# A hybrid trunk of two layers: bias sums and products with ones moved five matmuls up, and one matmul behind each widened to 258 columns

## The chip, the cores and the metric

The kernel runs on one core of a Trainium2 chip. The metric is the device time of one execution in microseconds (us). Three runs of the kernel before took 574.57, 574.65 and 574.93 us; the median is 574.65 us.

## The reference

Two layers work on 256 tokens of width 1024. Each layer is a token mixer with a residual, then an MLP with a residual, and each begins with an RMS norm. Layer 0 mixes by latent attention (MLA, 8 heads, rotary key), layer 1 by block-sparse attention (MoBA, here one block of 256 keys) with a relative bias from a table of 32 buckets. The MLP is `relu(h @ w_in)` squared, times `w_out`, with 4096 hidden columns.

```python
def sq_relu_mlp(h, w_in, w_out):
    a = jax.nn.relu(h @ w_in)
    return (a * a) @ w_out

for i in range(DEPTH):
    h = rms_norm(x, attn_norm[i])
    x = x + (mla_mixer(h, ...) if i % 2 == 0 else moba_mixer(h, ..., positions, rel_bias_table))
    h = rms_norm(x, mlp_norm[i])
    x = x + sq_relu_mlp(h, mlp_w_in[i], mlp_w_out[i])
```

The relative bias depends on positions and the table alone, so it can be computed at any time ahead of layer 1's attention.

## The kernel before, in words

**Arithmetic.** Weights and activations are float32. TensorE multiplies them as fp32r, in one pass, which keeps fewer bits; so each operand is split into a high part and the rest (`wh`, `wl` for weights, `hTh`, `hTl`, `a0`, `a1`, `aT0`, `aT1` for activations), and each product is three matmuls: high by high, rest by high, high by rest. This is `mm3` (lines 87 to 91), which calls `mm` (line 85, where the profile puts nearly all matmuls). ScalarE makes the high part (line 149), VectorE the rest (line 158), for units of 128x1024 of the weights that the DMA queue of SyncE brings in the order of use (line 138). `fill` asks for the next units, `done` gives one free.

**Layout.** Activations are kept transposed, 128 features by 256 tokens. In the MLPs and in the output projections of the attention the weight part (128x128) is the stationary operand, and the 256 tokens are the moving one, so each matmul has 256 columns and sums into a PSUM bank. In the projections ahead of the attention it is the other way: the tokens are stationary, and 512 columns of the weights (384 or 320 in the first) move.

**The attention's end.** `run_heads` computes eight heads and their output projection. The last three of its columns, `col(5)` to `col(7)`, run behind everything else: 3 x 8 heads x 3 = 72 matmuls of 256 columns each, one group of 24 after the other.

**The MLP.** `mlp` (line 870) runs twice over half of the hidden columns (`r`), and in each: eight times `first` (`j` from 0 to 7), which makes two blocks of 128 hidden columns with 2 x 8 `mm3` = 48 matmuls, then eight times an output block (`d`), 16 `mm3` = 48 matmuls into one bank. That makes 32 groups of 48 per MLP. Behind a group come `fill`, then what the list `fillers` has for that place (lines 890 and 931), then the reading of the bank: ScalarE and VectorE square it (lines 896 to 904), or VectorE scales it (line 936) and GpSimd adds it to the residual (line 938). An order is written by hand: each engine runs its instructions in the order in which the code gives them.

**What interrupts the fp32r matmuls in the MLP.** Two things. The RMS norm's sum over features is made with a product with a matrix of ones, in float32 (line 917), behind the group `r = 0, j = 6` of each MLP; its operand `s` is summed by GpSimd (lines 275 and 280). And during the MLP of layer 0 twelve blocks of layer 1's bias are made: `steps` (line 977, VectorE) compares positions with bucket limits, and one group later `sums` (lines 980 to 991) multiplies the comparisons `st` in eight bf16 matmuls of 96 columns with the table's differences in `parts3`, into two banks, from which VectorE adds them to `bias` (line 990). These twelve pieces stand behind the groups `d = 1` to `7` of the first half and, in the second half, behind `j = 0` (`first`), `j = 2` and `5`, and `d = 1` and `3`. The first of them runs at 150.7 us of the span, the last at 257.2.

Of the kernel before, what the change touches and what calls it, by code (L numbers as in the profile page):

```python
# [60 lines left out]
def trunk(ctx: ExitStack, tc: tile.TileContext, A, out):  # L61
# [9 lines left out]
    def ps():  # L71
        return psum.tile([P, 512], F32, name="ps", tag="ps")
# [11 lines left out]
    def mm(o, a, b, start, stop):  # L84
        nc.tensor.matmul(o, a, b, start=start, stop=stop)  # L85

    def mm3(o, a, b, start, stop):

        mm(o, a[0], b[0], start, False)
        mm(o, a[1], b[0], False, False)  # L90
        mm(o, a[0], b[1], False, stop)


    def flat(ap):
        return ap.rearrange("p a b -> p (a b)")
# [80 lines left out]
    def part(u, sl):  # L176
        return u[0][:, sl], u[1][:, sl]
# [352 lines left out]
    class Head:  # L530


        def __init__(self, hd, aT, h, bias, extra=None):
            self.aT = (aT[0][:, h], aT[1][:, h])
            self.i = h % HG
            self.hd = hd[h // HG]
            self.h, self.bias, self.extra = h, bias, extra
# [53 lines left out]
    def run_heads(hs, proj, post, rows, turn, mid, base, gname, n1):  # L591

        A_ = [h.logits for h in hs]
        W_ = [h.weights for h in hs]
        B_ = [h.turn for h in hs]
        C_ = [h.values for h in hs]
        accs = []

        def o(h, ds=range(4)):
            u = unit(base + h // 2)  # L600
            for d in ds:
                if h == 0:
                    accs.append(ps()[:, :S])
                c = (h % 2) * 512 + d * P
                mm3(accs[d], part(u, slice(c, c + P)), hs[h].aT, h == 0, h == H - 1)
                if h == H - 1:
                    out_residual(accs[d], d, gname)
            if h % 2:
                done(base + h // 2)

        late = {}

        def col(d, hh):
            if d not in late:
                late[d] = ps()[:, :S]
            u = unit(base + d)
            for h in hh:
                mm3(late[d], part(u, slice(h * P, (h + 1) * P)), hs[h].aT, h == 0, h == H - 1)
            if hh[-1] == H - 1:
                done(base + d)  # L620
                out_residual(late[d], d, gname)

        if mid is not None:
            proj("k1", 0)
            fill(n1)
            post("k1", 0)
            mid()
            proj("k1", 1)
            lo(n1)
            rows("k1", 0)  # L630
            hi(n1)
            post("k1", 1)
        A_[0]()
        proj("v1", 0)
        if mid is not None:
            lo(n1)
            rows("k1", 1)
        W_[0]()
        hi(n1)
        post("v1", 0)  # L640
        turn("k1", 0)
        A_[1]()
        if mid is None:
            rows("k1", 1)
        B_[0]()
        proj("v1", 1)
        lo(n1 + (mid is None))
        W_[1]()
        hi(n1)
        post("v1", 1)  # L650
        turn("k1", 1)
        C_[0]()
        A_[2]()
        B_[1]()
        proj("q1", 0)
        lo(n1)
        W_[2]()
        hi(n1)
        post("q1", 0)
        C_[1]()  # L660
        A_[3]()
        B_[2]()
        proj("q1", 1)
        lo(n1)
        W_[3]()
        rows("q1", 0)
        hi(n1)
        post("q1", 1)
        C_[2]()
        B_[3]()  # L670
        o(0)
        fill()
        turn("q1", 0)
        rows("q1", 1)
        C_[3]()
        o(1)
        fill()
        turn("q1", 1)
        o(2, range(2))
        A_[4]()  # L680
        o(2, range(2, 4))
        W_[4]()
        A_[5]()
        lo()
        o(3)
        B_[4]()
        hi()
        W_[5]()
        A_[6]()
        col(4, [0, 1])  # L690
        C_[4]()
        B_[5]()
        W_[6]()
        A_[7]()
        lo()
        col(4, [2, 3])
        C_[5]()
        B_[6]()
        hi()
        W_[7]()  # L700
        o(4)
        fill()
        C_[6]()
        B_[7]()
        o(5)
        fill()
        C_[7]()
        o(6)
        fill()
        col(4, [4, 5, 6])  # L710
        o(7)
        col(4, [7])
        for d in range(5, KD):
            col(d, range(H))
# [152 lines left out]
    mla_ctx.close()  # L867


    def mlp(l, base, fillers, finish):  # L870

        with tc.tile_pool(name=f"mlp{l}", bufs=1) as pool:
            scale = pool.tile([P, S], F32, name="scale")
# [1 line left out]
            a = [pool.tile([P, 2 * NPAIR, S], F32R, name=f"a{i}") for i in range(2)]  # L875
            sums = SumSquares()

            def first(b, r, j, split_k):
                u = [unit(b + 2 * j + i) for i in range(2)]
                if split_k:  # L880
                    o = [ps()[:, :S] for _ in range(2)]
                else:
                    p = ps()
                    o = [p[:, f * S:(f + 1) * S] for f in range(2)]
                for f, k in [(f, k) for k in range(KD) for f in range(2)] if split_k else \
                        [(f, k) for f in range(2) for k in range(KD)]:
                    c = (k % 4) * 256 + f * P
                    mm3(o[f], part(u[k // 4], slice(c, c + P)), hT(k), k == 0, k == KD - 1)
                fill(2)
                for g in fillers:  # L890
                    if g[0] == (r, j):
                        g[1]()
                for f, n in ((0, 1), (1, 1)) if split_k else ((0, 2),):
                    src = o[f] if split_k else p
                    rl = t2(n * S)
                    nc.scalar.activation(rl, src, AF.Relu)  # L896
                    sq = t2(n * S)
                    nc.vector.scalar_tensor_tensor(sq, src, 0.0, rl, op0=OP.max, op1=OP.mult)  # L898
                    if l == 1 and r == NR - 1:
                        sq3 = sq.rearrange("p (a b) -> p a b", b=S)  # L900
                        nc.vector.tensor_mul(sq3, sq3, scale[:, None, :].to_broadcast([P, n, S]))
                    ah, al = (i[:, 2 * j + f:2 * j + f + n].rearrange("p a b -> p (a b)") for i in a)
                    nc.scalar.copy(ah, sq)  # L903
                    nc.vector.tensor_sub(al, sq, f32(ah))  # L904
                done(b + 2 * j + 1)

            for r in range(NR):
                b = base + r * (2 * NPAIR + 2 * KD)
                for j in range(NPAIR):
                    first(b, r, j, r == 0 and j == 0)  # L910
                    if r == 0 and 1 <= j < 5:
                        sums.add(j - 1)
                    if r == 0 and j == 5:
                        s = sums.total()
                    if r == 0 and j == 6:
                        pb = ps()
                        mm(pb[:, :S], ones, s, True, True)
                        nc.vector.tensor_scalar(scale, pb[:, :S], 1.0 / D, EPS, op0=OP.mult, op1=OP.add)
                        nc.vector.reciprocal(scale, scale)
                b += 2 * NPAIR  # L920
                for d in range(KD):
                    o = ps()[:, :S]
                    for f in range(2 * NPAIR):
                        u = unit(b + 2 * d + f // 8)
                        c = (f % 8) * P
                        mm3(o, part(u, slice(c, c + P)), (a[0][:, f], a[1][:, f]), f == 0, f == 2 * NPAIR - 1)
                        if f == 7:
                            fill()
                            done(b + 2 * d)
                    fill()  # L930
                    for g in fillers:
                        if g[0] == (r, NPAIR + d):
                            g[1]()
                    if l == 0 or r < NR - 1:
                        y = t2(S)
                        nc.vector.tensor_tensor(y, o, scale, op=OP.mult)  # L936
# [31 lines left out]
    class BiasBlock:  # L968
# [9 lines left out]
                                    steps_k[:, k0 // 4:k0 // 4 + 8, None].to_broadcast([P, 8, P]), op=OP.is_ge)  # L978

        def sums(self):  # L980
            col = self.k0 if self.t == 0 else P + self.k0
            for h in range(2):
                pb = ps()
                for kk in range(4):
                    mm(pb[:, kk * 96:(kk + 1) * 96], self.st[:, 4 * h + kk], parts3, True, True)
                dst = bias[:, :, col + 16 * h:col + 16 * (h + 1)]
                src = pb[:, :384].rearrange("p (k i g h) -> p i h k g", i=3, g=4, h=H)
                for i in range(3):
# [18 lines left out]
        (nc.sync if d == KD - 1 else nc.gpsimd).dma_start(out[:, d], y)  # L1007

    blocks = [BiasBlock(i) for i in range(12)]
    fillers = [((0, 1), table_loads), ((0, 5), bias_tables)]  # L1010
    for i, b in enumerate(blocks):
        r, j = (0, NPAIR + i) if i < KD else (1, (1, 4, 8, 10)[i - KD])
        fillers += [((r, j), b.steps), ((r, j + 1) if j + 1 < 2 * NPAIR else (r + 1, 0), b.sums)]
    fillers.sort(key=lambda f: f[1].__name__ == "steps")
    mlp(0, M0, fillers, finish0)


    heads_ctx, hd1, aT1 = head_tiles(1)
# [71 lines left out]
    post1("v0", 1)  # L1090
    run_heads([Head(hd1, aT1, h, bias[:, h]) for h in range(H)], proj1, post1, rows1, turn1, lambda: turn1("q0", 1), O1, "mlp1", 2)
    heads_ctx.close()
    mlp(1, M1, [], finish1)


# [72 lines left out]
```

## Time and profile before

| | us |
|---|---|
| median of three runs | 574.65 |
| the profiled execution | 574.2 |
| its span, first to last instruction | 572.1 |
| TensorE matmuls busy | 566.0 |
| VectorE busy | 408.3 |
| ScalarE busy | 307.6 |
| the twelve bias sums, one after the other | 150.7 to 257.5 |
| product with ones, layer 0 and layer 1 | 133.3 and 426.9 |

Rows of the profile name the line, the engine, the operation, output<-inputs by the program's names, and shapes; a matmul `ps<-a,wh 128*128 128x256` moves 256 columns of `a` past a stationary 128x128 part of `wh`. A timeline row has the start, the length and a count (x2 where alike and overlapping instructions are merged). A matmul's length is longer than the distance to the next one, because matmuls are pipelined; so what a matmul costs is read from starts: count in a window, or the distance of two rows. PEclk is the clock that TensorE was granted, in tenths.

### The profile page before, as it was taken

How to read it: one execution, taken by the hardware profiler on the slowest of the kernel's cores; microseconds unless marked ns; L12 is line 12 of the kernel's file. 1: busy time of each engine (PE TensorE's matmuls, PEld its weight loads, DVE VectorE, ACT ScalarE, POOL GpSimd, SP SyncE). 2: the span in 40 equal slices, each digit the busy share in tenths (PEclk: the TensorE clock that was granted, in tenths of full speed). 3: DMA queues.
4: the chain of work that ended last, by engine and by line, in shares of the span. 5: the costliest groups of instructions: out<-in, count | busy, mean ns of one | idle time of the engine just before them, and what ended most of it. 6: DMA issues, size and time to landing. Idle time of an engine off the chain costs nothing.

```text
span 572.1 us, 10749 instructions
## 1 busy us (share of the span) xinstructions
PE 566.0 (99%) x4346; PEld 539.9 (94%) x4346; DVE 408.3 (71%) x654; ACT 307.6 (54%) x495; POOL 109.3 (19%) x105
## 2 busy tenths in 40 slices
PE   8999999999999999999999999999999999999997
PEld 6878999999999999999988888999999999999997
DVE  5997777588999978686648466776778555777531
ACT  6989666664433455444544566755664433555420
POOL 4882100040223100123413100000231322000100
PEclk9999999999999999999999999999999999999999
DMA  8834455554665555675636544345466666465730
GB/s 300 296 111 131 128 158 162 174 167 154 205 184 178 153 189 178 217 226 180 205 129 179 184 152 147 112 148 184 148 192 210 190 186 184 147 193 176 253 125 29
DMA packets 29186, 99.56 MB, mean 174 GB/s; under 512 B 3825, under 2 KB 4721, under 8 KB 29137
## 3 DMA queue, kind: packets, MB, share of 16 engines
q1 hardware_dynamic: 28656, 97.94, 53.9%
q0 software_dynamic: 336, 0.92, 0.4%
q8 instruction: 34, 0.56, 0.4%
q14 instruction: 16, 0.12, 0.1%
q10 hardware_dynamic: 144, 0.02, 0.0%
HBM read 97.82 MB, written 1.05 MB: 173 GB/s over the span
## 4 chain that ended last, share of the span: by engine, by line
PE 96%; DMA 2%; SPq 1%; issue 0%; DVE 0%; ACT 0%
PE ps L85 93%; PE ps L346 1%; DMA xs<-in_x_tok 1%; PE ps L569 1%; DMA win<-in_w_in 1%; SPq L138 0%; SPq L204 0%; PE ps L486 0%; DVE wl L158 0%; ACT wh L149 0%; DVE t L1006 0%; ACT sqj L451 0%; PE ps L851 0%
## 5 line engine op out<-in xcount | busy, mean ns | idle before, releaser
L149 ACT CAST wh<-raw 128x1024 fp32r<-128x1024 f32 x177 | 183.2, 1047 | 109.3 <-DMA raw<-in_w_out_mlp 55.7
L158 DVE TENSOR_TENSOR wl<-raw,wh 128x1024 fp32r<-128x1024 f32 x177 | 226.8, 1310 | 6.7 <-ACT wh L149 6.4
L85 PE MATMUL ps<-a,wh 128*128 128x256 f32 x1024 | 183.5, 280 | 0.0
L85 PEld LDWEIGHTS ps<-a,wh 128*128 128x128 f32 x1024 | 157.2, 188 | 0.0
L85 PE MATMUL ps<-hTh,wh 128*128 128x256 f32 x512 | 143.8, 281 | 0.0
L85 PE MATMUL ps<-hTh,wl 128*128 128x256 f32 x512 | 143.1, 279 | 0.0
L85 PE MATMUL ps<-a,wl 128*128 128x256 f32 x512 | 142.9, 279 | 0.0
L85 PE MATMUL ps<-hTl,wh 128*128 128x256 f32 x512 | 142.8, 279 | 0.0
L85 PEld LDWEIGHTS ps<-hTh,wh 128*128 128x128 f32 x512 | 96.2, 188 | 0.1
L85 PEld LDWEIGHTS ps<-hTl,wh 128*128 128x128 f32 x512 | 96.0, 188 | 0.0
L85 PEld LDWEIGHTS ps<-hTh,wl 128*128 128x128 f32 x512 | 95.9, 187 | 0.1
L85 PEld LDWEIGHTS ps<-a,wl 128*128 128x128 f32 x512 | 95.8, 187 | 0.0
L85 PE MATMUL ps<-aT,wh 128*128 128x256 f32 x256 | 51.0, 289 | 0.0
L85 PE MATMUL ps<-wh,hTh 128*128 128x512 f32 (+2 forms) x128 | 46.1, 385 | 1.6 <-DVE wh L420 1.1
L85 PE MATMUL ps<-wl,hTh 128*128 128x512 f32 (+2 forms) x128 | 45.1, 378 | 0.1
L85 PE MATMUL ps<-wh,hTl 128*128 128x512 f32 (+2 forms) x128 | 44.8, 377 | 0.0
L938 POOL TENSOR_TENSOR x<-t,x 128x256 f32<-128x256 f32 x16 | 26.4, 1649 | 94.4 <-DVE t L936 94.4
L903 ACT CAST a<-t 128x512 fp32r<-128x512 f32 (+1 forms) x34 | 20.2, 595 | 38.5 <-DVE t L898 26.4
L85 PEld LDWEIGHTS ps<-aT,wh 128*128 128x128 f32 x256 | 40.5, 188 | 0.2
L898 DVE SCALAR_TENSOR_TENSOR t<-ps,t 128x512 f32<-128x512 f32 (+1 forms) x34 | 22.3, 657 | 23.4 <-ACT t L896 23.4
L904 DVE TENSOR_TENSOR a<-t,a 128x512 fp32r<-128x512 f32 (+1 forms) x34 | 22.5, 661 | 22.5 <-ACT a L903 22.5
L85 PE MATMUL ps<-aT,wl 128*128 128x256 f32 x128 | 35.8, 280 | 0.0
(166 smaller groups left out, 631.1 us busy)
## 6 DMA issues: line engine op xcount, KB each, us to landing
raw<-in_w_in_mlp SPq DMA_DIRECT2D x64, 512.0 KB, 4.2
raw<-in_w_out_mlp SPq DMA_DIRECT2D x64, 512.0 KB, 4.1
raw<-in_w_qkv SPq DMA_DIRECT2D x24, 512.0 KB, 4.4
raw<-in_w_u SPq DMA_DIRECT2D x8, 512.0 KB, 6.2
win<-in_w_in SPq DMA_DIRECT2D x8, 352.0 KB, 5.3
raw<-in_w_o0a SPq DMA_DIRECT2D x4, 512.0 KB, 3.6
raw<-in_w_o0b SPq DMA_DIRECT2D x4, 512.0 KB, 3.9
raw<-in_w_o1a SPq DMA_DIRECT2D x4, 512.0 KB, 4.1
```

The costliest lines, as they stand in the source:

```text
L85: nc.tensor.matmul(o, a, b, start=start, stop=stop)
L149: (eng.copy if eng is nc.scalar else eng.tensor_copy)(his[i][:, :w], raws[i][:, :w])
L158: eng.tensor_sub(los[i][:, :w], raws[i][:, :w], f32(his[i][:, :w]))
L346: nc.tensor.transpose(pt[:, i * P:(i + 1) * P], yf[:, i * P:(i + 1) * P], ident)
L569: nc.tensor.transpose(pt[:, i * P:(i + 1) * P], self.p[:, i * P:(i + 1) * P], ident)
L898: nc.vector.scalar_tensor_tensor(sq, src, 0.0, rl, op0=OP.max, op1=OP.mult)
L903: nc.scalar.copy(ah, sq)
L904: nc.vector.tensor_sub(al, sq, f32(ah))
L938: nc.gpsimd.tensor_add(x[:, d], y, x[:, d])
```

## The change

`mm3` takes two new arguments. With `wide`, its first matmul gets other operands; with `between`, a function is called behind its first matmul. A helper `wider` gives the operands with 258 columns in place of 256: two more columns of the moving tile (the first two of the slab that follows it), and two more of the bank, which nobody reads. A flag `moved` is cleared by whatever runs under `other_type` (the bias sums and the products with ones) and set by `wider`.

```diff
-    def mm3(o, a, b, start, stop):
-
-        mm(o, a[0], b[0], start, False)
+    def mm3(o, a, b, start, stop, wide=None, between=None):
+
+        mm(*((wide[0], a[0], wide[1]) if wide else (o, a[0], b[0])), start, False)
+        if between:
+            between()
         mm(o, a[1], b[0], False, False)
         mm(o, a[0], b[1], False, stop)
...
+    moved = [True]
+
+    def wider(bank, b):
+        moved[0] = True
+        return bank[:, :S + 2], flat(b[:, :2])[:, :S + 2]
+
+    def other_type(f):
+        def run():
+            f()
+            moved[0] = False
+        return run
...
-                mm3(late[d], part(u, slice(h * P, (h + 1) * P)), hs[h].aT, h == 0, h == H - 1)
+                mm3(late[d][:, :S], part(u, slice(h * P, (h + 1) * P)), hs[h].aT, h == 0, h == H - 1,
+                    wider(late[d], hs[h].two) if (d, h) == (5, 0) else None)
...
-                    mm3(o[f], part(u[k // 4], slice(c, c + P)), hT(k), k == 0, k == KD - 1)
+                    wide = None
+                    if k == f == 0 and not moved[0]:
+                        wide = wider(p[f], hTh)
+                    mm3(o[f], part(u[k // 4], slice(c, c + P)), hT(k), k == 0, k == KD - 1, wide,
+                        between if (f, k) == (1, KD - 2) else None)
...
+                    between = inside.get((r, j))
+                    if r == 0 and j == 6:
+                        pb = ps()
+                        between = other_type(lambda: mm(pb[:, :S], ones, s, True, True))
+                    first(b, r, j, r == 0 and j == 0, between)
...
-                        pb = ps()
-                        mm(pb[:, :S], ones, s, True, True)
                         nc.vector.tensor_scalar(scale, pb[:, :S], 1.0 / D, EPS, op0=OP.mult, op1=OP.add)
...
-                        mm3(o, part(u, slice(c, c + P)), (a[0][:, f], a[1][:, f]), f == 0, f == 2 * NPAIR - 1)
+                        mm3(o, part(u, slice(c, c + P)), (a[0][:, f], a[1][:, f]), f == 0, f == 2 * NPAIR - 1,
+                            wider(bank, a[0]) if f == 0 and not moved[0] else None,
+                            inside.get((r, NPAIR + d)) if f == 2 * NPAIR - 2 else None)
...
         def sums(self):
+            self.pb = [ps() for _ in range(2)]
+            for h in range(2):
+                for kk in range(4):
+                    mm(self.pb[h][:, kk * 96:(kk + 1) * 96], self.st[:, 4 * h + kk], parts3, True, True)
+
+        def add(self):
...
-        fillers += [((r, j), b.steps), ((r, j + 1) if j + 1 < 2 * NPAIR else (r + 1, 0), b.sums)]
+        place = (r, j + 1) if j + 1 < 2 * NPAIR else (r + 1, 0)
+        fillers += [((r, j), b.steps), (place, b.add)]
+        inside[place] = other_type(b.sums)
```

The eight sums of a block and the product with ones are no longer issued behind a group but inside it, behind the first matmul of its last `mm3` but one; five matmuls of the group are left behind them. VectorE's additions (`add`) stay where they were. The next group's first matmul, the sixth behind the switch, is widened. So are the first matmul of `col(5)` in both layers; that one is the 37th behind the last float32 matmul of the attention.

TensorE at the first bias block (MLP of layer 0, `d = 1` and `d = 2`), in the order before, from the last of the eight sums. `parts_1315` is the table's differences, `a_1321` and `a_1322` the high and low parts of the activations:

```order
L85 LDWEIGHTS st
L85 MATMUL ps<-parts_1315,st 128x96
L85 MATMUL ps<-a_1321,wh 128x256
L85 MATMUL ps<-a_1321,wl 128x256
L85 MATMUL ps<-a_1322,wh 128x256
L85 MATMUL ps<-a_1321,wh 128x256
L85 MATMUL ps<-a_1321,wl 128x256
```

The same place now:

```order
L85 LDWEIGHTS st
L85 MATMUL ps<-parts_1315,st 128x96
L85 MATMUL ps<-a_1321,wl 128x256
L85 MATMUL ps<-a_1322,wh 128x256
L85 MATMUL ps<-a_1321,wh 128x256
L85 MATMUL ps<-a_1321,wl 128x256
L85 MATMUL ps<-a_1322,wh 128x256
L85 MATMUL ps<-a_1321,wh 128x258
L85 MATMUL ps<-a_1321,wl 128x256
```

Five matmuls of `d = 1` now follow the sums, and the first of `d = 2` has 258 columns.

TensorE at the product with ones (`j = 6` and `j = 7`) before; `ssum` is the sum of squares:

```order
L85 MATMUL ps<-hTh,wh 128x256
L85 MATMUL ps<-hTh,wl 128x256
L85 MATMUL ps<-hTl,wh 128x256
L85 MATMUL ps<-ssum,ones 128x256
L85 MATMUL ps<-hTh,wh 128x256
L85 MATMUL ps<-hTh,wl 128x256
```

And now:

```order
L85 MATMUL ps<-hTh,wh 128x256
L85 MATMUL ps<-ssum,ones 128x256
L85 MATMUL ps<-hTh,wl 128x256
L85 MATMUL ps<-hTl,wh 128x256
L85 MATMUL ps<-hTh,wh 128x256
L85 MATMUL ps<-hTh,wl 128x256
L85 MATMUL ps<-hTl,wh 128x256
L85 MATMUL ps<-hTh,wh 128x258
```

The product stands five matmuls further up, and the first matmul of `j = 7` has 258 columns. In all, 16 matmuls are widened: one in each attention, one behind each product with ones, and one behind each of the twelve blocks of sums. On VectorE, ScalarE, GpSimd and SyncE's queue the order of instructions is the same in both kernels.

More of the change, by code (lines that the diff above doesn't have):

```diff
@@ L534, in __init__ @@
             self.aT = (aT[0][:, h], aT[1][:, h])
+            self.two = aT[0][:, :2]
             self.i = h % HG
@@ L614, in col @@
             if d not in late:
-                late[d] = ps()[:, :S]
+                late[d] = ps()
             u = unit(base + d)
             for h in hh:
-                mm3(late[d], part(u, slice(h * P, (h + 1) * P)), hs[h].aT, h == 0, h == H - 1)
+                mm3(late[d][:, :S], part(u, slice(h * P, (h + 1) * P)), hs[h].aT, h == 0, h == H - 1,
+                    wider(late[d], hs[h].two) if (d, h) == (5, 0) else None)
             if hh[-1] == H - 1:
                 done(base + d)
-                out_residual(late[d], d, gname)
+                out_residual(late[d][:, :S], d, gname)
         if mid is not None:
@@ L867, in trunk, with mlp @@
     mla_ctx.close()
-    def mlp(l, base, fillers, finish):
+    def mlp(l, base, fillers, inside, finish):
         with tc.tile_pool(name=f"mlp{l}", bufs=1) as pool:
@@ L876, in mlp, with run_fillers, first @@
             sums = SumSquares()
-            def first(b, r, j, split_k):
-                u = [unit(b + 2 * j + i) for i in range(2)]
[L880 to L884, printed above, removed]
+            def run_fillers(r, j):
+                for g in fillers:
+                    if g[0] == (r, j):
+                        g[1]()
+            def first(b, r, j, split_k, between=None):
+                u = [unit(b + 2 * j + i) for i in range(2)]
+                p = [ps() for _ in range(2 if split_k else 1)]
+                o = [p[f][:, :S] if split_k else p[0][:, f * S:(f + 1) * S] for f in range(2)]
                 for f, k in [(f, k) for k in range(KD) for f in range(2)] if split_k else \
@@ L887, in first @@
                     c = (k % 4) * 256 + f * P
-                    mm3(o[f], part(u[k // 4], slice(c, c + P)), hT(k), k == 0, k == KD - 1)
+                    wide = None
[3 more added lines that the diff above has]
+                        between if (f, k) == (1, KD - 2) else None)
                 fill(2)
-                for g in fillers:
-                    if g[0] == (r, j):
-                        g[1]()
+                run_fillers(r, j)
                 for f, n in ((0, 1), (1, 1)) if split_k else ((0, 2),):
-                    src = o[f] if split_k else p
+                    src = o[f] if split_k else p[0]
                     rl = t2(n * S)
@@ L909, in mlp @@
                 for j in range(NPAIR):
-                    first(b, r, j, r == 0 and j == 0)
+                    between = inside.get((r, j))
[3 more added lines that the diff above has]
+                    first(b, r, j, r == 0 and j == 0, between)
                     if r == 0 and 1 <= j < 5:
@@ L921, in mlp @@
                 for d in range(KD):
-                    o = ps()[:, :S]
+                    bank = ps()
+                    o = bank[:, :S]
                     for f in range(2 * NPAIR):
@@ L930, in mlp @@
                     fill()
-                    for g in fillers:
-                        if g[0] == (r, NPAIR + d):
-                            g[1]()
+                    run_fillers(r, NPAIR + d)
                     if l == 0 or r < NR - 1:
@@ L980, in sums @@
         def sums(self):
+            self.pb = [ps() for _ in range(2)]
[3 more added lines that the diff above has]
+        def add(self):
             col = self.k0 if self.t == 0 else P + self.k0
             for h in range(2):
-                pb = ps()
-                for kk in range(4):
-                    mm(pb[:, kk * 96:(kk + 1) * 96], self.st[:, 4 * h + kk], parts3, True, True)
+                pb = self.pb[h]
                 dst = bias[:, :, col + 16 * h:col + 16 * (h + 1)]
@@ L1009, in trunk @@
     blocks = [BiasBlock(i) for i in range(12)]
+    inside = {}
     fillers = [((0, 1), table_loads), ((0, 5), bias_tables)]
@@ L1012, in trunk @@
         r, j = (0, NPAIR + i) if i < KD else (1, (1, 4, 8, 10)[i - KD])
-        fillers += [((r, j), b.steps), ((r, j + 1) if j + 1 < 2 * NPAIR else (r + 1, 0), b.sums)]
+        place = (r, j + 1) if j + 1 < 2 * NPAIR else (r + 1, 0)
+        fillers += [((r, j), b.steps), (place, b.add)]
+        inside[place] = other_type(b.sums)
     fillers.sort(key=lambda f: f[1].__name__ == "steps")
-    mlp(0, M0, fillers, finish0)
+    mlp(0, M0, fillers, inside, finish0)
     heads_ctx, hd1, aT1 = head_tiles(1)
@@ L1092, in trunk @@
     heads_ctx.close()
-    mlp(1, M1, [], finish1)
+    mlp(1, M1, [], {}, finish1)
 def kernel(x, positions, rel_bias_table, attn_norm, mlp_norm, mla_w_in, mla_q_a_norm, mla_kv_a_norm,
```

## The prediction

> **What bounds the kernel now.** I read the page first: who is busy, at which granted clock, and what the chain that ended last is made of.
>
> ```profile
> span 572.1 us, 10749 instructions
> ...
> PE 566.0 (99%) x4346; PEld 539.9 (94%) x4346; DVE 408.3 (71%) x654; ACT 307.6 (54%) x495; POOL 109.3 (19%) x105
> ...
> PEclk9999999999999999999999999999999999999999
> ...
> PE 96%; DMA 2%; SPq 1%; issue 0%; DVE 0%; ACT 0%
> ```
>
> TensorE is busy for 99% of the span at the full granted clock, and 96% of the chain is TensorE's own work, one matmul behind another. The waits of PE say the same from the other side:
>
> ```profile
> PE ps L85 <- DVE wh L420: 1.1, 1, 1.1
> PE ps L85 <- DVE warm L192: 1.0, 1, 1.0
> PE ps L85 <- ACT wh L149: 0.5, 1, 0.5
> ```
>
> These are all of PE's waits, 2.6 us, and their partners (the warming, the first weights) lie in the kernel's first microseconds. So nothing that other engines do sets the time around the change; only the spacing of matmuls does. That spacing comes from windows with PE alone (length, busy us, matmuls that overlap the window):
>
> ```profile
> 84.00:130.00 46.00, 46.00 (x393) 1.00 0.57 174
> 152.00:156.00 4.00, 4.00 (x37) 1.00 0.36 137
> 432.00:560.00 128.00, 128.00 (x1089) 1.00 0.58 183
> ```
>
> A matmul of 256 columns is shown 0.28 us long while its successor starts after less than half of that, so about 2.4 of those counted began ahead of the window. 46.00/(393-2.4) = 0.1178 us, 128.00/(1089-2.4) = 0.1178 us, and within its coarser counting 4.00/(37-2.4) = 0.116. The fp32r matmuls of 256 columns run at 117.8 ns each, from the end of the attention to the end of the MLP.
>
> To see what these 117.8 ns are made of I need other lengths. First two pieces of the chain in layer 1's projections, pure 512-column streams (start, us, what):
>
> ```profile
> 304.12 5.60 PE ps L85 x24
> 310.16 11.20 PE ps L85 x48
> ```
>
> 5.60/24 = 11.20/48 = 0.2333 us. Between 256 and 512 columns lie 115.5 ns, so a column costs 0.4512 ns, and 117.8 - 115.5 = 2.3 ns are left for each matmul whatever its length. Is that fixed part always the same? The input projection alternates 384 and 320 columns; the timeline merges four to a row:
>
> ```profile
> 10.81 0.80 PE L85 MATMUL ps<-wl,hTh 128*128 128x320 f32 x4
> ...
> 16.57 0.80 PE L85 MATMUL ps<-wl,hTh 128*128 128x320 f32 x4
> ```
>
> From the first of these rows to the last are nine steps of four, 36 matmuls in 5.76 us, 160.0 ns each; 352 columns on average cost 158.8 ns, so here the fixed part is 1.2 ns. And a few matmuls of 384 columns alone:
>
> ```profile
> 20.68 0.51 PE L85 MATMUL ps<-wh,hTl 128*128 128x384 f32 x2
> 21.03 0.51 PE L85 MATMUL ps<-wl,hTh 128*128 128x384 f32 x2
> ...
> 21.95 0.51 PE L85 MATMUL ps<-wh,hTl 128*128 128x384 f32 x2
> 22.30 0.51 PE L85 MATMUL ps<-wl,hTh 128*128 128x384 f32 x2
> 22.64 0.49 PE L486 MATMUL ps<-ident,cq 128*128 128x128 f32 x3
> ```
>
> Three steps of two, 0.35 + 0.35 + 0.34 us: 173.3 ns each, all of it the 384 columns (rows to 10 ns leave 2 ns open). So the fixed part is about 0, 1.2 or 2.3 ns by how the lengths follow each other. It is not a constant of the matmul; it depends on how each one lies behind the last.
>
> **The change part by part.** First, the sums and products are moved. This is the first of the twelve switches to the bf16 bias sums, in the order before:
>
> ```profile
> 150.62 0.28 PE L85 MATMUL ps<-a,wh 128*128 128x256 f32 x1
> 150.74 0.51 PE L85 MATMUL ps<-parts,st 128*128 128x96 bf16 x8
> 151.07 0.37 PE L85 MATMUL ps<-a,wh 128*128 128x256 f32 x1
> 151.28 0.28 PE L85 MATMUL ps<-a,wl 128*128 128x256 f32 x1
> 151.40 0.40 PE L85 MATMUL ps<-a,wh 128*128 128x256 f32 x2
> ```
>
> Eight sums take 0.33 us, and the first fp32r matmul behind them takes 0.21 us to its successor in place of 0.118: 0.09 us for coming back. All of this stays, in number and kind; it only happens five matmuls (0.59 us) earlier, inside a group. I cost the move at 0. That a switch inside a group is dearer or cheaper than at its edge no row shows; I bound it by that 0.09 us, either way, for 12 sums and 2 products: 14 x 0.09 = 1.3 us up or down.
>
> Do the moved steps have their operands? Of the sums, `st` (the bias block's comparisons, VectorE) must be there; of the product with ones, `ssum` (GpSimd):
>
> ```profile
> 152.83 1.21 DVE L977 TENSOR_TENSOR st<-steps_q,steps_k 128x1024 bf16<-128x1024 f32 x1
> 157.20 0.29 DVE L990 TENSOR_TENSOR bias<-ps,mask 128x128 f32<-128x128 f32 x1
> ```
>
> The second block's `st` is done at 154.04, and the add that reads its sums starts at 157.20; eight sums (0.33 us) and their way out lie before that, so the sums stand near 156.8, and 156.2 when moved. Some 2 us are left, and the other blocks have the same distance of at least one group of 48 matmuls (5.65 us) between `st` and sums. For the product:
>
> ```profile
> 127.68 1.60 POOL L280 TENSOR_TENSOR ssum<-ssum 128x256 f32<-128x256 f32 x1
> 133.34 0.59 PE L85 MATMUL ps<-ssum,ones 128*128 128x256 f32 x2
> ```
>
> `ssum` is ready at 129.28, the product goes from 133.34 to 132.75: 3.5 us of cover. If that cover were gone, PE would stand still in order and all groups behind it; it isn't. VectorE, ScalarE, GpSimd and the DMA queue keep their order, and what VectorE waits for comes earlier, not later:
>
> ```profile
> 151.12 0.29 DVE L990 TENSOR_TENSOR bias<-ps,mask 128x128 f32<-128x128 f32 x1 [1.02 <-PE ps L85]
> ```
>
> Its 1.02 us of idling for the sums shrinks by up to 0.59 us, which buys nothing, since PE waits for none of it. The two PSUM banks of a block are now taken together; with the group's own that is three of eight per group, so a bank comes back after more than two groups, over 11 us.
>
> Second, 16 matmuls get two columns more (one in each layer's attention, one behind each product, twelve behind the sums): 16 x 2 x 0.4512 ns = 0.014 us. Their own cost is nothing; a hiccup like that of a switch, 0.09 us on each, would be 1.4 us, and nothing suggests one.
>
> Third, what they do to those behind them. From the first widened one on, every fp32r matmul of 256 columns up to the next switch comes two columns later against whatever made the 2.3 ns. How many are these? In each layer 3 late columns x 24 = 72, and 32 MLP groups x 48 = 1536, so 1608. Five behind each switch are not reached: 13 switches in layer 0, one in layer 1. 1608 - 65 + 1608 - 5 = 3146. So each nanosecond per matmul is 3.15 us of the kernel.
>
> The trace of before has no stream that was shifted by two columns. The bounds by its rows: the fixed part goes (as for 384 alone), 2.3 ns x 3146 = 7.2 us less; or it grows by as much as it was ever seen to differ, 1.1 ns, 3.5 us more; and nothing at all in between. I take 1.1 ns less, the step from the 2.3 ns of the pure streams to the 1.2 ns of the mixed one, because the mixed stream is the nearest row: the one longer stream where unequal lengths meet, in which the mean was lower, not higher. 3146 x 1.1 = 3.5 us.
>
> The sum, against the profiled execution's own 574.2 us (span 572.1 and 2.1 around it): 574.2 + 0.0 - 3.5 + 0.0 = 570.7. The median of the runs, 574.65, is 0.45 above that execution, so 571.2 to be measured.
>
> The Trainium skill, "TensorE: Matmul & The Clock Gate", section "Wait — 56ns, not 53.3ns?", speaks against the change: it gives a warm matmul N/2.4 GHz plus a fixed 2.5 ns, with no memory of what went before. The trace agrees only in part: 2.3 ns is near its fixed part, but 0.4512 ns per column is not its 0.4167, and 1.2 ns in the mixed stream is no constant. By that rule, the sum would be 574.2 + 0.01.
>
> **The rivals.** *The spacing has no memory: same.* A matmul's extra two columns are paid once, and the stream falls back to 117.8 ns. For this: the streams at 84:130 and at 432:560 follow different switches (one a value product of the attention, one the product with ones) and have the same spacing to 0.1 ns; and the 512-column stream seems to have two patterns with one mean:
>
> ```profile
> 283.03 0.39 PE L85 MATMUL ps<-wh,hTh 128*128 128x512 f32 x1
> 283.26 0.39 PE L85 MATMUL ps<-wh,hTl 128*128 128x512 f32 x1
> ...
> 310.47 0.39 PE L85 MATMUL ps<-wl,hTh 128*128 128x512 f32 x1
> 310.70 0.40 PE L85 MATMUL ps<-wh,hTh 128*128 128x512 f32 x1
> ```
>
> Around 283 all of them last 0.39 us, around 310 0.39 and 0.40 alternate, and still the second stream's mean is the 0.2333 us of above. So a stream does remember how it began, in its pattern, but the mean did not care. Against it: all fp32r lengths ahead of these streams are multiples of 64 columns, and a shift by two is one that this trace never shows. Time: 574.65 + 0.01, 574.7. Chance 0.33.
>
> *The two columns put the stream out of a step that it is in: slower.* If the 2.3 ns are a mean in which some of the matmuls fall into a free place and others pay, a shift can lose the free place. Place: the same 3146 matmuls. Price: 1.1 ns more each, the only difference that rows show, 3.5 us: 578.1. It decides from 0.37 ns per matmul on (1.15 us). For it: the same rows as for the gain, read the other way; against it: the streams with the least regular lengths had the smaller part. Chance 0.19.
>
> *The price per column falls too.* The bf16 sums take 0.33 us for 8 x 96 columns, 0.43 ns per column with everything, or 110 ns for 256. At that rate 7.8 ns x 3146 = 24.5 us go: 550. No fp32r stream in the trace comes near it. Chance 0.04.
>
> That the change does not do what it says (a widened matmul missing, a sum left behind) leaves 574.7, and is within the first rival.
>
> **How the numbers follow.** The forecast has 0.44: 571.2. Its own range is 567.5 (574.65 - 7.2, the whole fixed part gone) to 573.5, the edge of what can be told from no change (0.2%, 1.15 us, is about what a measurement of this kernel can tell). The range I give takes in the switches' 1.3 us below that, in part, and above no change: 566.5 to 576.2. Left out are the third rival (0.04), a gain of all 7.2 us with cheaper switches (0.02) and most of the slower rival (0.12): 0.18. Faster by over 0.2%: 0.44 + 0.04 = 0.48; within: 0.33; slower: 0.19.
>
> **What would show it.** In the profile after, the window 432:560 should hold about 128/0.1167 + 2.4 = 1099 matmuls; 1089 again means the first rival, 1080 or less the second. The five matmuls between a switch and the widened one should still run at 117.8 ns, and those behind it at 116.7: if the twelve stretches between sums gain as much per matmul as the long one of layer 1, the shift acts at once and lasts. Wrong would be a PE wait on `st` or `ssum` (the covers above), a first matmul behind a switch of more than 0.21 us (the move is dear), or a spacing that changes in layer 1 but not between sums (then place, and not the two columns, decides).

## The result, and the profile after

The changed kernel takes 567.37 us (median of four, 566.5 to 567.46) against 574.69 us before: a ratio of 0.9869, with a 95% interval of 0.9852 to 0.9886, so 7.3 us faster. The profiled execution took 567.46 us, with a span of 565.4.

TensorE is as busy and as little waiting as before; the page and the waits of PE show no new partner:

```profile
span 565.4 us, 10754 instructions
...
PE 560.3 (99%) x4346; PEld 534.9 (95%) x4346; DVE 407.3 (72%) x654; ACT 307.8 (54%) x495; POOL 108.4 (19%) x105
...
PEclk9999999999999999999999999999999999999999
```

```profile
PE ps L85 <- DVE warm L210: 1.0, 1, 1.0
PE ps L85 <- DVE wh L438: 0.7, 1, 0.7
```

PE's busy time fell by 5.7 us at the same number of matmuls. Where? Windows of PE alone (length, busy us, matmuls that overlap), first of the kernel before, then of the changed one: the end of the attention and the MLP's start, a stretch behind the product with ones of layer 0, one behind the tenth block of sums, and layer 1 behind its product.

```profile
87.00:131.00 44.00, 44.00 (x376) 1.00 0.55 166
134.00:143.00 9.00, 9.00 (x79) 1.00 0.50 154
...
223.00:243.00 20.00, 20.00 (x172) 1.00 0.60 204
428.00:566.00 138.00, 138.00 (x1174) 1.00 0.55 177
```

```profile
87.00:131.00 44.00, 44.00 (x391) 1.00 0.55 173
134.00:143.00 9.00, 9.00 (x79) 1.00 0.50 157
...
221.00:241.00 20.00, 20.00 (x179) 1.00 0.61 202
422.00:560.00 138.00, 138.00 (x1174) 1.00 0.55 178
```

With the 2.4 or 2.5 matmuls taken off that began ahead of a window, 44.00/(391-2.5) = 0.1133 us and 20.00/(179-2.5) = 0.1133, against 0.1178 in the same places before. Behind both products the count is the same as before to the matmul: 79 and 1174. So the long stretches have one of two spacings, **113.3 or 117.8 ns**, and none lies between. The widened matmul moved the stream from the one to the other at the end of both attentions and behind the bias sums (all blocks but the first), and it did nothing behind the two products with ones, although it stands there at the same place, the sixth.

This is the second block of sums, in the timeline of the changed kernel; the row at 156.36 holds a high-by-rest matmul and, behind it, the widened one:

```profile
155.47 0.51 PE L85 MATMUL ps<-parts,st 128*128 128x96 bf16 x8
155.80 0.37 PE L85 MATMUL ps<-a,wl 128*128 128x256 f32 x1
156.01 0.40 PE L85 MATMUL ps<-a,wh 128*128 128x256 f32 x2
156.24 0.28 PE L85 MATMUL ps<-a,wl 128*128 128x256 f32 x1
156.36 0.40 PE L85 MATMUL ps<-a,wh 128*128 128x256 f32 x2
156.60 0.28 PE L85 MATMUL ps<-a,wl 128*128 128x256 f32 x1
...
156.94 0.28 PE L85 MATMUL ps<-a,wl 128*128 128x256 f32 x1
```

The three up to and with it take 0.36 us (156.24 to 156.60), the three behind it 0.34 (156.60 to 156.94). The sums themselves take 0.33 us and the first matmul behind them 0.21, as before the change.

Counted over all stretches that run at 113.3 ns, there are 402 matmuls ahead of each product and 947 behind eleven of the twelve blocks, 1751 in all; at 4.44 ns each that is 7.8 us. The span shrank by 6.7. Most of the difference lies ahead of the change: this execution came 0.92 us later to the first widened matmul, the second one of the row that starts at 86.09 us; in the kernel before, that row starts at 85.17.

### The profile page after: what moved, and what is told of

It reads as the page before. It is cut to its first block, busy times and chain, and to the rows that moved or that the text cites. A ratio compares the mean times of both kernels' runs of the same rounds, so it can differ in the third digit from the quotient of the medians.

```text
span 565.4 us, 10754 instructions
## 1 busy us (share of the span) xinstructions
PE 560.3 (99%) x4346; PEld 534.9 (95%) x4346; DVE 407.3 (72%) x654; ACT 307.8 (54%) x495; POOL 108.4 (19%) x105
## 4 chain that ended last, share of the span: by engine, by line
PE 98%; DMA 1%; DVE 0%; SPq 0%; issue 0%
PE ps L85 96%; PE ps L364 1%; PE ps L588 1%; DMA win<-in_w_in 1%; PE ps L504 0%; DVE t L1037 0%; SPq L222 0%; DVE wh L438 0%; PE ps L871 0%
## 5 line engine op out<-in xcount | busy, mean ns | idle before, releaser
L85 PE MATMUL ps<-a,wh 128*128 128x256 f32 x1024 | 179.5, 279 | 0.0
L85 PE MATMUL ps<-hTh,wl 128*128 128x256 f32 x512 | 142.7, 279 | 0.0
L85 PE MATMUL ps<-hTh,wh 128*128 128x256 f32 (+1 forms) x512 | 142.2, 278 | 0.0
L85 PE MATMUL ps<-aT,wh 128*128 128x256 f32 (+1 forms) x256 | 50.4, 288 | 0.0
L262 POOL TENSOR_TENSOR hrs<-hss,mhalf 128x4 f32<-128x4 f32 (+1 forms) x18 | 23.2, 1297 | 65.5 <-DVE hss L339 48.8
```

Of the source, the lines that this page charges most:

```text
L262: nc.gpsimd.tensor_tensor(dst, t, mhalf[:, :n].rearrange("p (a b) -> p a b", b=t.shape[-1]) if len(t.shape) == 3 else mhalf[:, :n], op=OP.pow)
```

## The experiments

My theory after this result, the **step theory**: a stream of 256-column fp32r matmuls has two lasting spacings; two columns more in one matmul take it from 117.8 to 113.3 ns, but only at certain steps of the stream, and a switch of type sets it back. The rival, the **distance theory**: the widened matmul works wherever it is far enough behind a switch, and a float32 product needs more distance than the bf16 sums.

All kernels are the changed kernel with three tables, which say for each switch how many matmuls of the group are left behind it and how many columns the next group's first matmul gets more; with the values below it is the changed kernel. The place of the widened matmul behind a switch is the first number plus one.

```diff
+COL5 = {"mlp0": 2, "mlp1": 2}
+ONES = [(5, 2), (5, 2)]
+SUMS = [(5, 2)] * 12
...
+    def switch(f, left, more):
+        def run():
+            f()
+            extra[0] = more
+        return {47 - left: run}
```

**The move alone.** No matmul is widened.

```diff
+COL5 = {"mlp0": 0, "mlp1": 0}
+ONES = [(5, 0), (5, 0)]
+SUMS = [(5, 0)] * 12
```

> Sums and products moved five matmuls up as in the change, no matmul widened. If the widening alone makes the gain, the time is that of before, 574.7 us within 0.3, and every stretch runs at 117.8 ns. If the move has a part in it, stretches behind moved sums run at 113.3 and up to 4.2 us of the gain (947 matmuls x 4.44 ns) stay.

Measured: 574.58 us against 574.61, ratio 0.9999 (0.9989 to 1.0008). Its windows hold what those of before do at 117.8 ns:

```profile
87.00:131.00 44.00, 44.00 (x376) 1.00 0.52 165
```

```profile
430.00:560.00 130.00, 130.00 (x1107) 1.00 0.56 183
```

130.00/(1107-2.4) = 0.1177. Moving sums and products costs and brings nothing that can be told (the interval leaves 0.6 us either way); without the wider matmuls none of the 7.3 us is there.

**Column 5 alone.** Two widened matmuls in the whole kernel, sums and products in their old places.

```diff
+ONES = [(0, 0), (0, 0)]
+SUMS = [(0, 0)] * 12
```

> Only the first matmul of column 5 is widened in both attentions; sums and products stand where they stood before, nothing else is widened. If a switch sets the stream back, only the two stretches of 402 matmuls up to the products run at 113.3 ns: 2 x 408 x 4.44 ns = 3.6 us less than before, 571.1. If a moved stream stayed moved across switches, the later stretches would gain too, up to 14 us.

Measured: 571.11 us against 574.61, ratio 0.9937 (0.9922 to 0.9952): 3.5 us, where 3.6 were expected. The shift lasts for all 407 matmuls up to the product (five more than in the changed kernel, since the product stands at its old place), and behind the product the spacing is 117.8 ns again:

```profile
87.00:131.00 44.00, 44.00 (x391) 1.00 0.54 172
...
430.00:560.00 130.00, 130.00 (x1106) 1.00 0.56 181
```

So 2 widened matmuls make half of the gain, and the remaining 3.8 us come from those behind the sums, since those behind the products moved nothing.

**Twelve places in one run.** Each block of sums has its widened matmul at another place.

```diff
+ONES = [(4, 2), (6, 2)]
+SUMS = [(q, 2) for q in range(12)]
```

> The twelve blocks of sums are left at different distances, so that the widened matmul (258 columns) is the 1st, 2nd, ... 12th behind its switch; it is the 5th behind the product with ones in layer 0 and the 7th in layer 1. Step theory (the stream repeats every three matmuls, and the two columns must fall on one step of the three): about one stretch in three runs at 113.3 ns per matmul, the others at 117.8; from place 6 it would be places 3, 6, 9 and 12, and one of the products' places 5 and 7 could work. Distance theory (a widened matmul works once it is far enough behind a switch, farther behind a float32 product): all places from 6 on, or from some smaller number on, run at 113.3, the lower ones at 117.8, and layer 1's long stretch stays at 117.8 at place 7. If layer 1's stretch moves, the whole is about 5.3 us (1196 x 4.44 ns) faster than the changed kernel, less what the stretches at bad places lose, at most 4.2 us.

The windows lie behind the twelve blocks in their order (places 1 to 12), and behind the product of layer 1 (place 7):

```profile
149.50:154.00 4.50, 4.50 (x40) 1.00 0.51 183
155.50:160.00 4.50, 4.50 (x41) 1.00 0.57 188
161.50:166.00 4.50, 4.50 (x41) 1.00 0.57 185
167.60:172.10 4.50, 4.50 (x40) 1.00 0.59 178
173.70:178.20 4.50, 4.50 (x40) 1.00 0.50 145
179.60:184.10 4.50, 4.50 (x42) 1.00 0.57 175
185.60:190.10 4.50, 4.50 (x41) 1.00 0.53 159
191.70:196.20 4.50, 4.50 (x41) 1.00 0.52 160
203.50:208.00 4.50, 4.50 (x42) 1.00 0.47 171
220.30:224.80 4.50, 4.50 (x40) 1.00 0.50 185
243.30:247.80 4.50, 4.50 (x41) 1.00 0.72 244
255.00:259.50 4.50, 4.50 (x42) 1.00 0.47 173
424.00:560.00 136.00, 136.00 (x1157) 1.00 0.56 177
```

At 117.8 ns 4.5 us hold 40.6 matmuls, at 113.3 ns 42.2. The three windows with 42 are places 6, 9 and 12. Places 7, 8, 10 and 11 are farther off than 6 and do not work, so distance does not decide. The blocks that had them were moved at place 6 in the changed kernel, so it is not the block either. Place 3, which the step theory had on its list, did not work. Behind layer 1's product place 7 failed (136.00/(1157-2.4) = 0.1178); behind layer 0's, place 5 worked for a dozen matmuls, until a delay of some 10 ns, too short to be listed as a wait, set the stream back. The whole took 568.65 us. The distance theory has fallen; every third place from 6 on fits the step theory, and place 3 remains as a miss of it.

**Other widths.** At place 6 behind the sums, 4 to 64 columns more; behind the products 2, at places 4 and 8.

```diff
+ONES = [(3, 2), (7, 2)]
+SUMS = [(5, x) for x in (4, 6, 8, 10, 12, 14, 16, 20, 24, 32, 48, 64)]
```

> Place 6 behind each block of sums as in the changed kernel, but 4, 6, 8, 10, 12, 14, 16, 20, 24, 32, 48 and 64 columns more instead of 2; 258 columns at place 4 behind the product in layer 0 and at place 8 in layer 1. Shift theory (what counts is where the columns fall against something that repeats): some widths give 113.3 ns, others 117.8, with a period that shows (8, 16 or 24 columns). Longer-matmul theory (any matmul longer than its neighbours breaks the step): all twelve stretches run at 113.3.

None of the twelve widths moved its stretch. Behind 32 columns more, for example, 20 us hold 172 matmuls, as in the kernel before:

```profile
223.00:243.00 20.00, 20.00 (x172) 1.00 0.54 187
```

Behind layer 1's product, place 8 worked; place 4 in layer 0 did not. With the places above that makes 5 and 8 for a product, not 4, 6 and 7. But layer 1 was not faster to its end:

```profile
426.00:520.00 94.00, 94.00 (x832) 1.00 0.58 186
524.00:562.00 38.00, 38.00 (x325) 1.00 0.46 151
```

94.00/(832-2.5) = 0.1133, then 38.00/(325-2.4) = 0.1178. Between lies a wait of PE for the last activations of the second half, those of `j = 7`. ScalarE had stood 2.90 us for a weight's DMA ahead of the Relu of the group before (`j = 6`, at 514.67); the Relu of `j = 7` follows at 519.17, behind two more copies of weights. That the long wait made these activations late is read from this order; the run does not test it.

```profile
522.38 0.39 PE L88 MATMUL ps<-a,wh 128*128 128x256 f32 x1 [0.78 <-ACT a L928]
```

```profile
513.71 1.05 ACT L169 CAST wh<-raw 128x1024 fp32r<-128x1024 f32 x1 [2.90 <-DMA raw<-in_w_out_mlp]
514.67 0.59 ACT L921 ACTIVATE t<-ps 128x512 f32<-128x512 f32 x1
...
519.17 0.59 ACT L921 ACTIVATE t<-ps 128x512 f32<-128x512 f32 x1
```

Behind the wait this stream had 117.8 ns to its end. The run took 568.79 us.

**Three places for four widths.** So that a width cannot fail for its place alone.

```diff
+ONES = [(4, 2), (4, 2)]
+SUMS = [(q, x) for x in (26, 18, 10, 4) for q in (8, 9, 10)]
```

> Behind the sums three places each (9, 10 and 11) for 26, 18, 10 and 4 columns more, so that no width can miss its step for want of the right place; place 5 behind the products. If the fast stream comes from where the columns fall against something that repeats every 24, 16 or 8 columns, 26, or 18, or 18 and 10 columns work at one place of three as 2 do, and 4 do not. If only a delay of a single matmul's step by two columns does it, none works. Place 5 behind the product should move layer 1's stretch as it did layer 0's: 113.3 ns.

None of the twelve stretches moved; of all widths, only 2 columns have. Place 5 behind layer 1's product worked: its window 426 to 520 us again holds 832 matmuls, 113.3 ns each. 568.07 us for the whole. What the three places do not exclude is said below.

**Place 8 behind both products.** The sums as in the change.

```diff
+ONES = [(7, 2), (7, 2)]
```

> The changed kernel with the products with ones seven instead of five matmuls up, so that the widened matmul is the 8th behind them in both layers; sums as in the change. Step theory: place 8 is a working step behind a product, so the stretch of about 130 matmuls in layer 0 and the one of 1198 in layer 1 run at 113.3 ns: 1328 x 4.44 ns = 5.9 us less than the changed kernel, about 561.5 us; with the 1.5 us wait that layer 1 showed behind a faster stream and the stream set back there, some 563 us. Distance theory: the same, since place 8 was seen to work once; the chance theory (place 8 worked by accident of timing): 567.4, as the changed kernel.

Measured: 563.33 us against 574.32, ratio 0.9809 (0.9795 to 0.9822): a gain of 11.0 us, where the change as it was made had 7.3. Layer 1 runs at 113.3 ns up to the second half's output blocks, and at 117.8 from there:

```profile
422.00:517.00 95.00, 95.00 (x841) 1.00 0.59 191
519.00:557.00 38.00, 38.00 (x325) 1.00 0.45 150
```

**Widened again.** As the run before, with three more widened matmuls in layer 1, at the first matmuls of d = 2 and d = 5 of the first half and of j = 0 of the second.

```diff
+AGAIN = [(1, 0, 10), (1, 0, 13), (1, 1, 0)]
+ONES = [(7, 2), (7, 2)]
```

> As the run before, and in layer 1 three more matmuls of 258 columns in a stream that runs at 113.3 ns already: first of the groups d = 2 and d = 5 of the first half and j = 0 of the second, each a multiple of 48 matmuls behind the first widened one. Step theory with columns that add up: the second takes the stream out again (117.8 ns), as four columns at once did, and later ones may or may not bring it back. State theory (the widened matmul puts the stream into a lasting state whatever it was): all pieces stay at 113.3 ns.

Four windows, behind the product and behind each of the three:

```profile
421.00:429.00 8.00, 8.00 (x73) 1.00 0.46 152
437.00:452.00 15.00, 15.00 (x130) 1.00 0.65 212
453.50:468.50 15.00, 15.00 (x130) 1.00 0.61 182
471.00:517.00 46.00, 46.00 (x408) 1.00 0.52 171
```

That is 113.5, 117.6, 117.6 and 113.4 ns by the count, which is coarse in short windows: in, out, still out, in again. The columns are not a switch that is thrown once: the second widened matmul took the stream out of the 113.3 ns spacing, and the fourth brought it back. It looks as if each shifted the stream by one step of three. The run took 563.88 us.

**Keeping the stream in step, first attempt.** In the groups j = 7, both the weights' copies (ScalarE) and subtractions (VectorE) go behind the squaring, for earlier activations; then also the norm's scale behind j = 7.

```diff
-                fill(2)
+                if j < NPAIR - 1:
+                    fill(2)
...
+                if j == NPAIR - 1:
+                    fill(2)
```

> The run with place 8 behind the products, and in the group j = 7 of each half the weights' next two units are prepared behind the squaring of that group instead of ahead of it, so that the activations for d = 0 are there earlier. If the wait of some 0.3 us at d = 0 sets layer 1's stream back to 117.8 ns, taking that wait away keeps the last 341 matmuls at 113.3: 341 x 4.44 ns + 0.3 us = 1.8 us less than with place 8 alone (563.3), 561.5 us. If the stream falls back there for another reason, 563.0. If the weights become late instead, PE waits for them and it is slower than 563.3.

```diff
-                    if r == 0 and j == 6:
+                    if r == 0 and j == 7:
                         nc.vector.tensor_scalar(scale, pb[:, :S], 1.0 / D, EPS, op0=OP.mult, op1=OP.add)
```

> As the run before, and the norm's scale (two VectorE operations, one of them a reciprocal of 1.75 us) is made behind j = 7 instead of j = 6. If the short delays of 0.02 to 0.1 us in layer 0, 13 and 91 matmuls behind the product, set that stretch back, it stays at 113.3 ns now: 126 x 4.44 ns + 0.2 us = 0.8 us less than the run before, and 0.2 more if the first block of sums then moves too: 560.6 us. If not, 561.5.

Measured: 572.29 us (ratio 0.9961, 0.9948 to 0.9975) and 573.32 us (0.9980, 0.9969 to 0.9990). Both expectations of a gain missed; the stated other outcome came. The subtractions make `wl`, and PE waited for it four times (from the first of the two runs):

```profile
PE ps L88 <- DVE wl L178: 5.4, 4, 1.7
```

The waits cost their own 5.4 us and the step as well: behind the first one in layer 1 the stream ran at 117.8 ns (84 us from 433 on hold 716 matmuls).

**Second attempt.** Only ScalarE's copies go behind the squaring; then, again, the scale too.

```diff
-                fill(2)
+                lo(2)
+                if j < NPAIR - 1:
+                    hi(2)
...
+                if j == NPAIR - 1:
+                    hi(2)
```

> Place 8 behind the products (563.3 us), and in the groups j = 7 only ScalarE's two copies of the next weights go behind the squaring, while VectorE's two subtractions stay ahead of it. ScalarE then no longer waits for a weight's DMA ahead of the squaring. If that wait is what makes the activations late at d = 0 in layer 1, the 0.3 us wait goes and the stream's last 341 matmuls stay at 113.3 ns: 561.5 us. If weights are late instead, as with both moved, PE waits on wl and the time is over 563.

> As the run before, with the norm's scale made behind j = 7 instead of j = 6. If the reciprocal causes the short delay 13 matmuls behind the product in layer 0, that stretch keeps 113.3 ns to its end: 0.6 to 0.8 us less than the run before, 560.8. If the scale then makes the weights of d = 0 late, it loses more than that, as a wait of 1.4 us did.

Measured: 562.24 us (ratio 0.9789, 0.9768 to 0.9810) and 561.18 us (0.9779, 0.9754 to 0.9804). In the profiled execution of the first, layer 1 kept its step from the product to the end:

```profile
421.00:554.00 133.00, 133.00 (x1176) 1.00 0.57 183
```

133.00/(1176-2.5) = 0.1133; this execution took 560.57 us. In layer 0 it shows something else. The stream behind the product was set back after a dozen matmuls, as with place 8 alone, and later came to 113.3 ns again without any wider matmul: at 142.7 us two steps of the stream were longer, 0.13 and 0.22 us in place of 0.118, and behind them 4.5 us hold 42 matmuls. With place 8 alone the same two steps were 0.22 us each, and the stream stayed at 117.8 ns.

```profile
136.00:142.00 6.00, 6.00 (x53) 1.00 0.46 156
143.50:148.00 4.50, 4.50 (x42) 1.00 0.74 248
```

So a short delay can do what the two columns do, and its length matters. That suggests that a shift of the stream in time is what counts, and that the wider matmul is one way to make it.

In the second run, layer 0 has 113.3 ns behind the product to the end of the stretch (14.00/(126-2.5) = 0.1134):

```profile
133.00:147.00 14.00, 14.00 (x126) 1.00 0.63 208
...
518.00:554.00 36.00, 36.00 (x320) 1.00 0.48 159
```

That the later scale did this is not shown. The delay that the expectation names came too early for it: in the first run the step at 133.51 is the long one (0.13 us), and the scale's first operation on VectorE starts 2.9 us later.

```profile
133.51 0.29 PE L88 MATMUL ps<-hTh,wl 128*128 128x256 f32 x1
133.64 0.28 PE L88 MATMUL ps<-hTl,wh 128*128 128x256 f32 x1
```

```profile
136.40 0.42 DVE L949 TENSOR_SCALAR scale<-ps 128x256 f32<-128x256 f32 x1
```

Up to there both kernels have the same order of instructions, so its absence in the second run does not come from the edit. The scale can bear only on the delay at 142.7, which was missing too.

In layer 1 of the second run PE waited again for the activations, 0.9 us at 515, and this time the stream had 113.3 ns behind the wait (36.00/(320-2.5) = 0.1134). Ahead of the Relu of `j = 6`, where this edit changes nothing, ScalarE had stood 3.10 us for a weight's DMA; in the first run the wait at that place was 1.15 us. So the edit alone does not keep the activations in time.

```profile
507.92 1.05 ACT L169 CAST wh<-raw 128x1024 fp32r<-128x1024 f32 x1 [3.10 <-DMA raw<-in_w_out_mlp]
```

The single runs of both kernels spread from 560.3 to 564.4 us, more than the two differ by, and those with place 8 alone from 562.6 to 564.2; the intervals of the ratios overlap, so a gain over place 8 alone is not clear. Both beat the kernel before by 12 to 13 us and the change as made by 5 to 6.

## Why the prediction was half right

I forecast 571.2 us, 3.5 us less than before; measured were 567.37, 7.3 us less.

**Right: what bounds the kernel.** Only the spacing of matmuls counts; no wait came with the change, and what was costed at nothing (the move, the 16 wider matmuls themselves) is nothing that can be told: 574.58 against 574.61 us for the move without widening, 0.21 us for the first matmul behind a switch as before, and 0.12 us from the widened one behind layer 1's product to its successor.

**Right: the direction and the kind.** The two columns are paid once and the spacing behind them is lower for hundreds of matmuls, with the attention's end and the stretches between sums gaining the same per matmul. The first rival (no memory) has fallen, by the 402 matmuls at 113.3 ns behind a single widened one. Yet the sign that I had named for it came: the window 432:560 holds 1089 matmuls after the change as before. It lies in the one long stretch that the change did not reach, so one window was a poor sign for the whole kernel. The second rival's picture, a stream in a step that two columns can take it out of, was the right picture; its sign was wrong for the state that the streams were in, and right for a stream at 113.3 ns, as the run that widens again shows. Why the streams of the kernel before were at 117.8 ns and not at 113.3, nothing in the prediction said.

**Wrong: the term "3146 x 1.1 = 3.5 us", in both factors.** *The gain per matmul* was 4.44 ns and not 1.1. I read 117.8 and 233.3 ns as 0.4512 ns per column and a fixed 2.3 ns, and let the fixed part be all that could go. At that price 256 columns alone would take 115.5 ns; the moved stream takes 113.3 for the whole matmul, at most 0.4426 ns per column (113.3/256). So the line through two lengths gave neither the price of a column nor a fixed part that bounds the gain, and the mixed stream of 384 and 320 columns was no row to scale by. The third rival named the price per column, but took its size from bf16. The Trainium skill, "TensorE: Matmul & The Clock Gate", section "Wait — 56ns, not 53.3ns?", has one spacing per length for a warm matmul, 256/2.4 + 2.5 = 109.2 ns as an estimate by it; the runs show 117.8 and 113.3 at the full granted clock, and its rule holds for neither.

*The number of matmuls* was 1751 and not 3146. The step that failed says that "every fp32r matmul of 256 columns up to the next switch" comes under the shift behind a widened one. Behind both products and behind the first block it did not: the widened matmul was there and had no effect. I had taken the place as a detail; by the run with twelve places it decides. 1199 of the lost matmuls are layer 1's. The two errors pull opposite ways: 1751 x 4.44 = 7.8 us, where 3146 x 4.44 would have been 14.0 us and a time of some 561, below my range. That the measured time lies inside the range is luck.

**Missed: what is late next.** I counted on no new wait, and as far as the change reaches there is none. When the stream of layer 1 is faster too (place 8), PE comes to the second half's output blocks ahead of the last activations, and the wait there can cost the step as well as the time.

**What stays open.** What in the hardware has the two spacings, and why every third place works, the runs do not show. Behind the sums each place other than 6 was tried once, and place 3 missed. Nor is it excluded that other widths work: that three neighbouring places cover all steps was assumed, and delays without any wider matmul had the same effect. Why the first block of sums was not moved in the changed kernel, but was in the last two runs, was not settled. In the changed kernel and in four more runs with place 6 there, the stream ahead of this block ran at 117.8 ns and the block did not move; in the last two it ran at 113.3 and the block moved. But the second block moved in the changed kernel behind a stretch at 117.8 ns, so that alone does not decide.

## What to carry to other kernels

When matmuls run back to back, read their spacing by stretches to a tenth of a nanosecond before looking for waits: here nearly 4% of it depended on how the stream had begun, at the same clock and with no listed wait. Do not split such a spacing into a price per column and a fixed part from two lengths alone. An edit that shifts a stream is to be tried at several places at once, and every stretch read by itself, since one total time hides that some stretches gained all and others nothing.

## What the runs showed of the hardware

- fp32r matmuls of 256 columns run at 117.8 or at 113.3 ns in this kernel, each stably for over 1100 matmuls at the full granted clock. Of the fifteen extra widths tried (2 to 64 columns), only 2 led from the one to the other.
- 258 columns worked at places 6, 9 and 12 behind bf16 sums (1 to 12 were tried) and at 5 and 8 behind a float32 product (4 to 8 were tried), and at no other of these.
- Behind bf16 sums or a float32 product every stream ran at 117.8 ns at first, also where it had run at 113.3 ahead of them.
- Delays of PE shift a stream too. In layer 1 the wait for the last activations set it back from 113.3 to 117.8 ns in all profiled executions shown that had one, except the last; in layer 0 of the first run of the second attempt, a delay of some 0.1 us took it from 117.8 to 113.3.
